# A Winograd-tiled pooling mixer: the first two products read inputs that are not yet normalized, and the second phase's weight operands are formed where they are needed

## The chip, the cores and the metric

The kernel runs on one core of a Trainium2 chip. A core has a matrix engine (TensorE, PE in the profile; PEld is its weight load), a vector engine (VectorE, DVE), a scalar engine (ScalarE, ACT), a general engine (GpSimd, POOL) that only issues transfers here, and a sync engine (SyncE, SP) that issues most of them. The engines run side by side and wait for one another through semaphores; each takes its own instructions in the order in which they were written for it. Matmul results land in eight PSUM banks of 128 x 512 floats, everything else lies in SBUF. The metric is the time of one execution in microseconds (us), as the median of several runs.

## The reference

One layer is computed (`DEPTH = 1`), the pooling mixer, on 4096 tokens of 1024 channels in float32:

```python
def pool_mixer(h, in_w, group_w, group_b, scale, out_w):
    u, gate = jnp.split(h @ in_w, 2, axis=-1)
    ug = u.reshape(b, s, POOL_GROUPS, POOL_GROUP_DIM)
    pooled = jnp.stack([trailing_mean(ug[:, :, g], w) for g, w in enumerate(POOL_WINDOWS)],
                       axis=2) - ug
    mixed = jnp.einsum('bsgc,gcd->bsgd', pooled, group_w) + group_b
    y = mixed.reshape(b, s, POOL_WIDTH) * scale * jax.nn.silu(gate)
    return y @ out_w

out = rms_norm(x + pool_mixer(rms_norm(x, norm_w), ...), final_norm_w)
```

`rms_norm` divides each token by the root of its mean square and multiplies by a weight per channel. `in_w` is 1024 x 2048 (a half for `u`, a half for the gate), `out_w` 1024 x 1024; there are four groups of 256 channels, with trailing windows of 2, 4, 8 and 16 tokens.

## The kernel before

**The arithmetic.** The factor per token of the first norm (here: the scale) is kept apart from the weight per channel, which is multiplied into the rows of `in_w`. The map of each group commutes with the mean over tokens, so it is folded into the `u` half of `in_w` once, at the start (`fold`, L284: `in_w` transposed times `group_w`, eight calls of 16 matmuls). Then the kernel has three phases, all made of blocked products in Winograd's form, seven products where plain blocking has eight:

- Phase a: 4 blocks of 1024 tokens, columns of groups 0 and 1. The input block is 2 x 2 (two halves of 512 tokens, two halves of the channels, called 11, 12, 21, 22), the weight is 2 x 2 (two halves of the channels; gate columns and folded columns).
- Phase b: the same blocks, columns of groups 2 and 3.
- Phase o: 8 blocks of 512 tokens times `out_w`, then the final norm.

A step is one product P1 to P7 of one block: 56 steps of 48 matmuls in phases a and b (order P1 P2 P6 P7 P5 P4 P3), 56 of 24 in phase o. Each float32 operand is split into a rounded high part (copied by ACT, L151) and a low part (subtracted by DVE, L145), and each product of two 128 x 128 by 128 x 512 blocks takes three matmuls (`mm3`, L457). The split input of a step lies in two of four `op` tiles, so a split can be made once the step before the last has been read out. P1 and P2 sum in the banks 0 to 3; P1 alone is also needed, so its four banks are copied to the banks 4 to 7 in between (`evict_in`, L564, ACT).

**The start.** SP loads the sources of the fold, then rows of `x` for the scales, then the transposed blocks. `square_row` (L316, ACT) gives the mean squares and `stats` (L325) four scales per partition for 512 tokens. `spread_rs` (L338) brings them to every partition: DVE forms a diagonal matrix in a weight tile not yet in use, two matmuls with ones (L351) write the bank 7, ACT copies it out. `normalize` (L365, DVE) multiplies an input half by it; then it is split, and GpSimd stores it, since phase b reads it again (`sd`).

**Later blocks.** For block b+1 the rows are loaded and squared during block b; the scales go to DRAM (`rd`) and come back broadcast to all partitions (`store_rs`, `load_rstd`), on the queue of SP. Pooling (`pool`, L503) is DVE work of one to four adds per group.

**Weights of phase b.** During blocks 1 and 2 of phase a, after P5, `make_wb` (L239) loads the gate rows of `in_w` and the folded weights `wvd`, forms all seven operands of one channel quarter pair (ACT scales, five DVE operations) and stores them in DRAM (`wbd`, 7 stores of 512 KB per call). After each product of the last block, `load_w` (L257) loads that product's operand for phase b from `wbd` and splits it into the weight tiles just set free.

**What sets the order.** The Python text gives the work in order of steps; a framework then places the instructions of all engines by its own estimates of time, keeping each engine's queue in the resulting order. `tc.high_priority()` moves a part ahead, `tc.issue_after(i)` holds one behind an instruction. Tiles for loads and temporaries come from two pools with the oldest free tile taken first (`Slots`), so a transfer waits for whoever read its tile last.

Of the kernel before, what the change touches and what calls it, by code (L numbers as in the profile page):

```python
# [60 lines left out]
def kernel(  # L61
# [91 lines left out]
    def split(dst, src):  # L153
# [3 lines left out]

    colt = const.tile([P, 24], F32, name="colt")
# [7 lines left out]
    wbd = {  # L166
        i: [dram.tile([P, 2, H], F32, name=f"wbd{i}_{h}") for h in range(2)]
        for i in range(P1, P7 + 1)
    }
# [270 lines left out]
    def split_in(q, b, i):  # L440
        s = xs[b]
        key = {P1: "11", P2: "12", P6: "2", P7: "21", P5: "11", P4: "22", P3: "12"}[i]
        t = split_halves(s[key], None if q else sd[b].get(i), b == 0)
# [5 lines left out]
        return t  # L449

# [15 lines left out]
    def product_in(i, t, sets, by_bank, between=None):  # L466
# [4 lines left out]
        for n, (h, ct) in enumerate(halves):  # L471
            if n == 5 and between:
                between()
# [90 lines left out]
    def evict_in(b, q, i, sets):  # L564
        ps = sets[bank_of[i]]
        last = None
        if i == P1:
# [282 lines left out]
    ru[0, 4] = load_wut(0, 4)  # L850
    g0.append(load_rows(in_w, 0, D))
    ru[0, 2] = load_wut(0, 2)
    g0.append(load_rows(in_w, 2, D))
    load_row(0, 0, 0)
    load_row(0, 0, 1)
    ru[0, 6] = load_wut(0, 6)
    load_row(0, 0, 2)
    load_row(0, 0, 3)
    ident = take(pool=early)
    nc.sync.dma_start(out=ident.rearrange("p a b -> p (a b)")[:, 0:P], in_=eye)  # L860
    gw[1] = load_group_w(1)
    v0, v1 = [None] * 2, [None] * 2
    for n, (h, k) in enumerate(chunks):
# [16 lines left out]
    give(gw[0])  # L880
    for h, k in chunks[1:]:
        ru[1, k] = load_wut(1, k)
# [14 lines left out]

    for n, (h, k) in enumerate(chunks):
        o = take(pool=early if n < 2 else early5)
        last = fold(1, k, gw[1], ru[1, k], banks[2 * (n % 2) : 2 * (n % 2) + 2], o)  # L900
# [193 lines left out]
```

## Time and profile before

| what | value |
|---|---|
| median of 3 runs (range) | 971.4 us (971.11 to 971.44) |
| the profiled execution: its time, its span | 973.14 us, 971.0 us |
| PE / PEld busy | 951.5 / 786.4 us |
| DVE / ACT / POOL busy | 745.6 / 452.2 / 6.7 us |
| granted TensorE clock, mean | 0.997 |
| read, written in DRAM | 116.50 MB, 67.12 MB |
| SP's queue, ACT's queue, GpSimd's queue (moved) | 163.71, 13.65, 6.29 MB |

The span is the time between the first and the last instruction; some 2 us of an execution lie around it. "Busy" counts overlapping instructions once, and matmuls are pipelined (one lasts 389 ns, but one ends every 227 ns in the even stretches), so a short wait of PE shows less idle time than it costs; the count of matmuls in a stretch tells more. A row of the timeline is: start, duration, engine, line, operation, output<-inputs, shape, count, and in brackets the idle time of the engine before it and what ended it.

### The profile page before, as it was taken

The numbers are of one execution on the slowest core, as the hardware profiler recorded it, in microseconds if no ns is written. First come the engines' busy times: TensorE is split into PE (matmuls) and PEld (weight loads), VectorE is DVE, ScalarE is ACT, GpSimd is POOL, SyncE is SP. The second block draws the span as 40 slices with busy tenths as digits, with TensorE's granted clock in tenths as the row PEclk, the third lists the DMA queues.
The fourth block names the chain that finished last, engine by engine and source line by source line (L and its number), as shares of the span: only waits on it lengthen the run. The fifth ranks groups of instructions, "written<-read, shape, count | busy, mean of one in ns | idle before, by whom it ended". The sixth has DMA issues, their size and how long they took to land.

```text
span 971.0 us, 11079 instructions
## 1 busy us (share of the span) xinstructions
PE 951.5 (98%) x4190; PEld 786.4 (81%) x4190; DVE 745.6 (77%) x907; ACT 452.2 (47%) x679; POOL 6.7 (1%) x16
## 2 busy tenths in 40 slices
PE   8899999989999999999999999999999999999996
PEld 7778888878877888888888888888888888888885
DVE  5696993886899794497598499599978677677675
ACT  4759438337545554345444435553424324324233
POOL 0100000000000000000000000000000000000000
PEclk9999999999999999999999999999999999999998
DMA  9964865977977624115714714646646446356022
GB/s 340 411 271 141 265 246 186 339 274 220 333 251 245 210 93 146 44 44 182 273 44 158 267 75 147 222 151 195 225 155 227 131 151 217 111 194 216 22 87 87
DMA packets 68933, 184.35 MB, mean 190 GB/s; under 512 B 6928, under 2 KB 24464, under 8 KB 68880
## 3 DMA queue, kind: packets, MB, share of 16 engines
q1 hardware_dynamic: 62976, 163.71, 49.1%
q10 hardware_dynamic: 4176, 13.65, 3.5%
q0 software_dynamic: 1728, 6.29, 1.6%
q8 instruction: 33, 0.54, 0.2%
q14 instruction: 20, 0.16, 0.1%
HBM read 116.50 MB, written 67.12 MB: 189 GB/s over the span
## 4 chain that ended last, share of the span: by engine, by line
PE 75%; DMA 10%; DVE 8%; ACT 4%; issue 1%; SPq 0%; ACTq 0%; DVEq 0%
PE bank L460 73%; DMA st<-in_in_w 3%; DMA rd<-rs 2%; DMA st<-rd 2%; DVE op L145 2%; PE bank L289 1%; DMA wbd<-vt 1%; DVE vt L142 1%; ACT vt L320 1%; DVE st L145 1%; DVE st L148 1%; DMA wbd<-st 1%; DMA early<-in_wut 1%; DVE st L546 1%; DVE vt L148 1%
## 5 line engine op out<-in xcount | busy, mean ns | idle before, releaser
L460 PE MATMUL bank<-op,w 128*128 128x512 f32 x2688 | 612.0, 389 | 5.6 <-DVE op L145 4.7
L460 PEld LDWEIGHTS bank<-op,w 128*128 128x128 f32 x2688 | 504.1, 188 | 112.7 <-DVE op L145 7.0
L460 PE MATMUL bank<-w,op 128*128 128x512 f32 (+1 forms) x1356 | 305.0, 387 | 0.0
L460 PEld LDWEIGHTS bank<-w,op 128*128 128x128 f32 x1356 | 253.1, 188 | 51.9
L151 ACT ACTIVATE op<-st 128x1024 fp32r<-128x1024 f32 x121 | 127.7, 1057 | 148.6 <-PE bank L460 108.2
L145 DVE TENSOR_TENSOR op<-st,op 128x1024 fp32r<-128x1024 f32 x121 | 147.3, 1223 | 58.9 <-ACT op L151 58.7
L142 DVE TENSOR_TENSOR vt<-vt 128x1028 f32<-128x1028 f32 (+6 forms) x72 | 88.0, 1235 | 1.7 <-DMA wbd<-vt 1.6
L151 ACT ACTIVATE op<-vt 128x1024 fp32r<-128x1024 f32 x45 | 47.4, 1059 | 81.1 <-PE bank L460 68.6
L142 DVE TENSOR_TENSOR st<-bank,st 128x512 f32<-128x512 f32 x76 | 52.0, 689 | 36.4 <-PE bank L460 34.3
L151 ACT ACTIVATE vt<-bank 128x512 f32<-128x512 f32 x94 | 54.8, 594 | 35.8 <-PE bank L460 34.2
L142 DVE TENSOR_TENSOR vt<-bank,vt 128x512 f32<-128x512 f32 (+1 forms) x85 | 56.7, 679 | 15.1 <-PE bank L460 8.7
L145 DVE TENSOR_TENSOR op<-vt,op 128x1024 fp32r<-128x1024 f32 x45 | 54.9, 1223 | 14.7 <-ACT op L151 14.6
L145 DVE TENSOR_TENSOR w<-st,w 128x1024 fp32r<-128x1024 f32 x32 | 39.1, 1224 | 21.4 <-ACT w L151 21.2
L151 ACT ACTIVATE w<-st 128x1024 fp32r<-128x1024 f32 x32 | 33.7, 1060 | 38.0 <-PE bank L460 28.7
L151 ACT ACTIVATE bank<-bank 128x512 f32<-128x512 f32 x48 | 27.9, 582 | 46.3 <-PE bank L460 29.9
L145 DVE TENSOR_TENSOR st<-st,st 128x1024 f32<-128x1024 f32 x38 | 46.2, 1224 | 2.4 <-DMA st<-wvd 1.9
L148 DVE TENSOR_TENSOR st<-st,st 128x1024 f32<-128x1024 f32 (+1 forms) x22 | 25.4, 1175 | 26.5 <-DMA st<-rd 18.3
L151 ACT ACTIVATE st<-bank 128x512 f32<-128x512 f32 x36 | 20.5, 594 | 20.0 <-DMA yd<-st 10.8
L541 DVE SCALAR_TENSOR_TENSOR vt<-vt,vt 128x1024 f32<-128x1024 f32 x24 | 29.4, 1226 | 0.1
L289 PE MATMUL bank<-early,early 128*128 128x256 f32 x128 | 28.3, 380 | 1.1 <-DVE st L297 1.1
L289 PEld LDWEIGHTS bank<-early,early 128*128 128x128 f32 x128 | 24.2, 190 | 4.7 <-DVE st L297 1.5
L142 DVE TENSOR_TENSOR st<-st,st 128x1024 f32<-128x1024 f32 x21 | 25.4, 1226 | 0.1
(109 smaller groups left out, 415.8 us busy)
## 6 DMA issues: line engine op xcount, KB each, us to landing
st<-in_x SPq DMA_DIRECT2D x32, 512.0 KB, 4.5
st<-sd SPq DMA_DIRECT2D x29, 512.0 KB, 4.5
vt<-in_x SPq DMA_DIRECT2D x27, 512.0 KB, 4.9
st<-in_xt SPq DMA_DIRECT2D x20, 512.0 KB, 5.9
st<-yd SPq DMA_DIRECT2D x19, 512.0 KB, 4.1
yd<-st SPq DMA_DIRECT2D x17, 512.0 KB, 3.5
out<-st SPq DMA_DIRECT2D x17, 512.0 KB, 5.1
sd<-st ACTq DMA_DIRECT2D x16, 512.0 KB, 5.6
```

The lines of the kernel that those rows point to most:

```text
L142: nc.vector.tensor_tensor(out=dst, in0=a, in1=b, op=ALU.add)
L145: nc.vector.tensor_tensor(out=dst, in0=a, in1=b, op=ALU.subtract)
L148: nc.vector.tensor_tensor(out=dst, in0=a, in1=b, op=ALU.mult)
L151: return nc.scalar.activation(dst, src, func)
L289: nc.tensor.matmul(ps2[kk][:, j * 256 : (j + 1) * 256], r[:, kk, 2 * j + t, :], g[:, 2 * j + t, :], start=(t == 0), stop=(t == 1),)
L320: nc.scalar.activation(u[:, 0], u[:, 0], AF.Square, accum_out=sums[b, half][:, j : j + 1])
L460: nc.tensor.matmul(ps, a, b, start=start and n == 0, stop=stop and n == 2, skip_group_check=True)
L541: nc.vector.scalar_tensor_tensor(out=s[:, :, at : at + H], in0=s[:, :, at : at + H], scalar=1.0 / win, in1=v[:, :, HIST:], op0=ALU.mult, o ...
L546: nc.vector.scalar_tensor_tensor(out=sg[:, j], in0=s[:, j, at : at + H], scalar=bias_c[2 * grp + j], in1=sg[:, j], op0=ALU.add, op1=ALU.mult,)
```

## The change

It has two parts, and some loads and squares of the start are put in another order with them.

1. In block 0 the inputs of P1 and P2 (11 and 12) are split as they are loaded (`raw`). The products are multiplied by the scales of the tokens when the banks are read out (`evict_in`: DVE multiplications in place of ACT copies; P2's sum then goes through the SiLU on ACT in two more operations). The inputs are normalized and stored afterwards (`normalize_raw`), for the products that need sums of them. The scales are spread at two points within the first product's text. All fold results are read out by ACT, none by DVE, and the transposed inputs are loaded ahead of the rows of `x`.
2. `wbd` is gone. For each product of phase b, `load_wb` loads the sources (gate rows, folded weights) one step ahead and `make_wb` forms and splits the operand in the steps 23 to 29, that is from P6 of the last block of phase a to P2 of the first of phase b. Sums are formed again where two products need them.

```diff
+    def split_negative(dst, src):
+        nc.scalar.activation(dst[:, 0], src, AF.Copy, scale=-1.0)
+        nc.vector.scalar_tensor_tensor(
+            out=dst[:, 1], in0=src, scalar=-1.0, in1=dst[:, 0].bitcast(F32),
+            op0=ALU.mult, op1=ALU.subtract,
+        )
...
-    def make_wb(h):
-        g0 = load_rows(in_w, 2 * h, D + H)
-        g1 = load_rows(in_w, 4 + 2 * h, D + H)
-        v0, v1 = take(), take()
-        nc.sync.dma_start(out=v0, in_=wvd[h])
-        nc.sync.dma_start(out=v1, in_=wvd[2 + h])
-        scale_rows(g0, pair(norm_c, h, 0))
-        scale_rows(g1, pair(norm_c, h, 1))
-        store_weights(wbd, h, g0, g1, v0, v1)
+    parts, t2 = {}, {}
+
+    def load_wb(i):
+        for h in range(2):
+            p = parts[i, h] = {}
+            if i in (P1, P6, P5):
+                p["11"] = load_rows(in_w, 2 * h, D + H)
+            if i in (P2, P4):
+                p["21"] = load_rows(in_w, 4 + 2 * h, D + H)
+            for name, k, used in (("12", h, (P6, P7, P5)), ("22", 2 + h, (P6, P7, P3))):
+                if i in used:
+                    p[name] = take()
+                    nc.sync.dma_start(out=p[name], in_=wvd[k])
+
+    def scaled(u, cs, other, op):
+        for j in range(2):
+            nc.vector.scalar_tensor_tensor(
+                out=u[:, j], in0=u[:, j], scalar=cs[j], in1=other[:, j], op0=ALU.mult, op1=op
+            )
+
+    def make_wb(i):
+        for h in range(2):
+            p = parts.pop((i, h))
+            top, bottom = pair(norm_c, h, 0), pair(norm_c, h, 1)
+            if i == P1:
+                split_scaled(w[i][h], p["11"], top)
+            elif i == P2:
+                split_scaled(w[i][h], p["21"], bottom)
+            elif i == P6:
+                sub(p["12"], p["22"], p["12"])
+                scaled(p["11"], top, p["12"], ALU.add)
+                t2[h] = p.pop("11")
+                split(w[i][h], t2[h])
+            elif i == P7:
+                sub(p["22"], p["22"], p["12"])
+                split(w[i][h], p["22"])
+            elif i == P5:
+                scaled(p["11"], top, p["12"], ALU.subtract)
+                split_negative(w[i][h], p["11"])
+            elif i == P4:
+                scaled(p["21"], bottom, t2[h], ALU.subtract)
+                split(w[i][h], p["21"])
+                give(t2.pop(h))
+            else:
+                split(w[i][h], p["22"])
+            for u in p.values():
+                give(u)
...
-            if q == 0:
+            if q == 0 and b > 0:
                 for u in s["11" if i == P1 else "12"]:
                     normalize(b, 0, u)
...
-        t = split_halves(s[key], None if q else sd[b].get(i), b == 0)
+        raw = b == 0 and i in (P1, P2)
+        t = split_halves(s[key], None if q or raw else sd[b].get(i), b == 0)
...
+    def normalize_raw(i):
+        for h, u in enumerate(xs[0]["11" if i == P1 else "12"]):
+            normalize(0, 0, u)
+            nc.gpsimd.dma_start(out=sd[0][i][h], in_=u)
...
-            if n == 5 and between:
-                between()
+            if between and n in between:
+                between[n]()
...
+        if i in (P1, P2) and b == 0 and q == 0:
+            if i == P2:
+                ev["11"] = [take() for _ in range(2)]
+            for c, u in enumerate(sets["y"] if i == P1 else cells(ev["11"])):
+                mul(u, ps[c], rstd[0][:, 0])
+            if i == P2:
+                for u in ev["11"]:
+                    last = copy(u, u, AF.Silu)
+        elif i == P1:
...
-        fold(0, k, gw[0], ru[0, k], banks[2 * (n % 2) : 2 * (n % 2) + 2], o, True)
+        fold(0, k, gw[0], ru[0, k], banks[2 * (n % 2) : 2 * (n % 2) + 2], o)
+        ru[1, k] = load_wut(1, k)
         if n == 0:
-            ru[1, 0] = load_wut(1, 0)
             load(0)
+            g0.append(load_rows(in_w, 2, D))
+            split_scaled(w[P1][0], g0[0], pair(norm_c, 0, 0))
         elif n == 1:
-            for hh in range(2):
-                split_scaled(w[P1][hh], g0[hh], pair(norm_c, hh, 0))
+            split_step(0)
         elif n == 2:
-            for j in range(4):
-                square_row(0, 0, j)
-            with tc.high_priority():
-                rs = stats(0, 0)
+            split_scaled(w[P1][1], g0[1], pair(norm_c, 1, 0))
+        if n > 1:
+            for j in range(2 * n - 4, 2 * n - 2):
+                load_row(0, 0, j)
...
-        if n == 1:
-            with tc.high_priority():
-                spread_rs(0, rs)
-            form(0)
-            split_step(0)
-            second_side(0)
-        elif n == 2:
-            behind = last.ins
+        if n < 2:
+            second_side(n)
+            for j in range(2 * n, 2 * n + 2):
+                square_row(0, 0, j)
+            if n == 1:
+                with tc.high_priority():
+                    rs[0] = stats(0, 0)
+        else:
+            for j in range(2 * n - 4, 2 * n - 2):
+                square_row(0, 1, j)
...
-    run(0, spread_second)
+    run(0, {1: lambda: spread(0), 5: lambda: spread(1)})
...
+    normalize_raw(P1)
+    for h in range(2):
+        for key in ("21", "22"):
+            normalize(0, 1, xs[0][key][h])
     form(2)
+    split_step(2)
     run(1)
-    split_step(2)
+    normalize_raw(P2)
...
+        since = n - (NB - 1) * len(ORDER_IN) - 2
+        if 0 <= since < len(ORDER_IN):
+            with tc.issue_after(evicted[0]):
+                make_wb(ORDER_IN[since])
+        if 0 <= since + 1 < len(ORDER_IN):
+            load_wb(ORDER_IN[since + 1])
...
-            if b == NB - 1:
-                load_w(wbd if kind == "a" else wod, i)
-            if i == P5:
-                if kind == "a" and b in (1, 2):
-                    make_wb(b - 1)
-                elif kind == "b" and b in (1, 2):
-                    make_wo(b - 1)
+            if kind == "b" and b == NB - 1:
+                load_w(wod, i)
+            if kind == "b" and b in (1, 2) and i == P5:
+                make_wo(b - 1)
```

More of the change, by code (lines that the diff above doesn't have):

```diff
@@ L165 @@
     wvd = [dram.tile([P, 2, H], F32, name=f"wvd{k}") for k in range(4)]
[L166 to L169, printed above, removed]
     wod = {
@@ L849 @@
     ru[0, 0] = load_wut(0, 0, by=1)
-    ru[0, 4] = load_wut(0, 4)
+    for h, k in chunks[1:]:
+        ru[0, k] = load_wut(0, k)
     g0.append(load_rows(in_w, 0, D))
[L852 to L858, printed above, removed]
+    gw[1] = load_group_w(1)
     ident = take(pool=early)
     nc.sync.dma_start(out=ident.rearrange("p a b -> p (a b)")[:, 0:P], in_=eye)
-    gw[1] = load_group_w(1)
     v0, v1 = [None] * 2, [None] * 2
@@ L896, in second_side, with spread @@
         split(w[P6][h], g0[h])
+    rs = [None] * 2
     for n, (h, k) in enumerate(chunks):
         o = take(pool=early if n < 2 else early5)
-        last = fold(1, k, gw[1], ru[1, k], banks[2 * (n % 2) : 2 * (n % 2) + 2], o)
+        fold(1, k, gw[1], ru[1, k], banks[2 * (n % 2) : 2 * (n % 2) + 2], o)
         nc.gpsimd.dma_start(out=wvd[k // 2], in_=o)
         give(o)
-        if n == 1:
-            with tc.high_priority():
-                spread_rs(0, rs)
-            form(0)
-            split_step(0)
-            second_side(0)
-        elif n == 2:
-            behind = last.ins
+        if n < 2:
[8 more added lines that the diff above has]
+                square_row(0, 1, j)
     give(gw[1])
     load(2)
-    with tc.issue_after(behind):
-        for j in range(4):
-            square_row(0, 1, j)
     with tc.high_priority():
-        rs = stats(0, 1)
-    def spread_second():
+        rs[1] = stats(0, 1)
+    def spread(half):
         with tc.high_priority():
-            spread_rs(1, rs)
-    run(0, spread_second)
+            spread_rs(half, rs[half])
+    run(0, {1: lambda: spread(0), 5: lambda: spread(1)})
     give(ident)
-    form(1)
     split_step(1)
```

6 lines of the change are left out of this document (1 added, 5 removed).

## The prediction

> **What bounds the kernel now.** I read the page first, then busy time by stretches, then PE's timeline of the stretches where it falls behind, then the queues that it waited for there. The page's first rows:
>
> ```profile
> span 971.0 us, 11079 instructions
> PE 951.5 (98%) x4190; PEld 786.4 (81%) x4190; DVE 745.6 (77%) x907; ACT 452.2 (47%) x679; POOL 6.7 (1%) x16
> ```
>
> PE is the bound, and the question is how often it falls behind. Busy time by stretches (PE's count in the first bracket):
>
> ```profile
> 39.70:60.00 20.30, 19.74 (x87) 15.81 (x85) 17.02 (x25) 13.89 (x23) 3.23 (x7) 1.00 1.03 416
> 60.00:140.00 80.00, 79.82 (x351) 65.30 (x350) 71.94 (x85) 48.40 (x74) 0.26 (x1) 1.00 0.62 207
> 39.70:320.00 280.30, 274.10 (x1200) 224.33 (x1199) 227.13 (x264) 161.77 (x254) 3.50 (x7) 1.00 0.75 259
> 320.00:960.00 640.00, 640.00 (x2826) 530.10 (x2825) 488.48 (x585) 264.24 (x381) 0.00 (x0) 1.00 0.43 149
> ```
>
> From 320 us on PE is never idle: 640/2826 = 0.2265 us per matmul, 10.87 us per step of 48. At that pace the 1200 matmuls of 39.7 to 320 need 271.8 us and took 280.3: 8.5 us lost, of which 0.6 before 60 us (87 need 19.7), 0.5 in 60 to 140 (351 need 79.5), so some 7.4 in 140 to 320. Nothing after 320 can get faster by this change. What it can reach is the time to the first product, these 8.5 us, and what it puts in anew. PE's timeline of the start:
>
> ```profile
> 7.30 13.97 PE L289 MATMUL bank<-early,early 128*128 128x256 f32 x64
> ...
> 22.38 3.69 PE L289 MATMUL bank<-early,early 128*128 128x256 f32 x16 [1.10 <-DVE st L297]
> 29.00 0.50 PE L351 MATMUL bank<-w,w 128*128 128x512 f32 x1 [2.94 <-DVE w L344]
> ...
> 30.00 10.09 PE L289 MATMUL bank<-early,early 128*128 128x256 f32 x46
> 39.74 9.00 PE L460 MATMUL bank<-op,w 128*128 128x512 f32 x38
> 49.29 0.50 PE L351 MATMUL bank<-w,w 128*128 128x512 f32 x1 [0.56 <-DVE w L344]
> ```
>
> The second half of the fold waits 1.1 us for an eviction by DVE, then 2.9 us at the spread of the scales. The later waits:
>
> ```profile
> 129.40 12.78 PE L460 MATMUL bank<-op,w 128*128 128x512 f32 x55 [0.18 <-DVE op L145]
> ...
> 198.24 12.30 PE L460 MATMUL bank<-op,w 128*128 128x512 f32 x53 [1.89 <-DVE op L145]
> 211.50 3.74 PE L460 MATMUL bank<-op,w 128*128 128x512 f32 x15 [0.96 <-ACT bank L151]
> ...
> 287.56 11.18 PE L460 MATMUL bank<-op,w 128*128 128x512 f32 x48 [2.06 <-DVE op L145]
> 299.30 3.94 PE L460 MATMUL bank<-op,w 128*128 128x512 f32 x16 [0.56 <-DVE op L145]
> ```
>
> They stand where blocks 2 and 3 begin. The recorded idle of the last four is 5.5 us. What DVE, ACT and SP did ahead of the first two (third column: engine; in brackets the idle time):
>
> ```profile
> 165.85 2.36 DVE L148 TENSOR_TENSOR st<-st,st 128x1024 f32<-128x1024 f32 x2 [6.82 <-DMA wbd<-st]
> 184.48 0.15 DVE L148 TENSOR_TENSOR rs<-rs,tmp 128x4 f32<-128x4 f32 x1
> 205.83 1.23 DVE L148 TENSOR_TENSOR st<-st,st 128x1024 f32<-128x1024 f32 x1 [3.10 <-DMA st<-rd]
> 210.86 0.58 ACT L151 ACTIVATE bank<-bank 128x512 f32<-128x512 f32 x1 [7.86 <-DMA sd<-vt]
> ```
>
> and, from the chain of waits, the two transfers that bring scales back:
>
> ```profile
> 192.11 6.54 DMA rd<-rs
> 198.71 7.09 DMA st<-rd
> ```
>
> DVE stands 6.8 us before a normalization because the scales come back through SP's queue in between `make_wb`'s loads and stores; its own operations then pile up; the next scales are ready at 184.6, leave at 192.1 and are back at 205.8; DVE waits for them again, ACT's stores of the results block ACT's copies of the banks, and PE waits for those.
>
> **The change part by part. Start.** Durations that I use:
>
> ```profile
> 22.08 1.28 ACT L186 ACT_TABLE_LOAD   x1
> 34.25 1.38 ACT L301 ACTIVATE early<-bank,colt 128x512 f32<-128x512 f32 x2
> 44.12 1.04 ACT L151 ACTIVATE op<-vt 128x1024 fp32r<-128x1024 f32 x1
> 48.25 0.19 ACT L151 ACTIVATE hl<-rs 128x4 fp32r<-128x4 f32 x1
> 49.76 1.41 DVE L206 SCALAR_TENSOR_TENSOR w<-st,colt,w 128x512 fp32r<-128x512 f32 x2
> 59.24 2.35 DVE L145 TENSOR_TENSOR early<-vt,st 128x1024 f32<-128x1024 f32 x2
> 77.95 3.12 ACT early L320 x6
> L142 DVE TENSOR_TENSOR st<-bank,st 128x512 f32<-128x512 f32 x76 | 52.0, 689 | 36.4 <-PE bank L460 34.3
> ```
>
> (A square with its sum: 3.12/3 = 1.04; a DVE operation of 1024 columns every 1.14 to 1.18, one of 512 with a scalar 0.7; a bank read by DVE 0.69, or 0.62 in a row, by ACT 0.6 to 0.7.)
>
> Removed from the path: nothing but evictions stands between the halves of the fold, and ACT makes these in time (two banks are always free). The first 64 fold matmuls end at 7.30 + 13.97 = 21.3, 0.218 each, 3.5 a fold; 64 more end at 35.2, so the first product starts at about 35.0 instead of 39.74: 4.7 us won. Its operands: the raw halves and the weights are loaded ahead of `x`, and their splits stand on ACT and DVE inside the first fold half, where DVE has lost its eight evictions.
>
> Put in its place: in the changed order of instructions the first spread stands on PE behind only 6 product matmuls, at 36.4 us. Its scales: the squares of the four rows stand on ACT between the fold's evictions, the last behind the second bank of the third fold of the second half (21.3 + 3 x 3.5 = 31.8; eviction to 32.4; square to 33.45); one more eviction to 34.2, a table load to 35.5, root and five small DVE operations at 0.2 to 36.8, the copy `hl` behind one more square at 36.95; from that copy to the spread matmul it was 49.29 - 48.25 = 1.04. So 38.0: PE waits 1.6, and 0.35 for the second spread matmul. From there DVE is one chain without a pause: the second spread matmul (0.5) ends at 39.2, ACT's copy of the bank (0.6) at 39.9, and until the sums for P6 stand two normalizations, four banks, two splits, the second spread, four half weight splits and small ones (12.8 us, to 52.7), then four normalizations and three sums (8.0, to 60.7); ACT's copy makes the operand of P6 ready at 61.9. PE has ended P2 at 38.9 + 89 x 0.2265 + 0.2 = 59.3, so it waits some 2.5 us, and 0.7 for the low part. P7 and P5 are met (0.1). Waits in all: 1.6 + 0.35 + 0.2 + 2.5 + 0.7 + 0.1 = 5.45. End of P5 after: 35.0 + 242 x 0.2265 + 5.45 = 95.3; before: 87 matmuls at 60.0 and 155 more, 95.1. The start gains 4.7 and gives it back: I take +0.4. Bounds: -3 if P6 does not wait; +3 if the scales take from the last square to the spread what they take now (the table load behind the last square began at 22.08, the spread at 29.0: 6.9 instead of my 4.55). The stores of the normalized halves move behind the fold's on GpSimd's queue; they are first read in phase b, and only DVE's later sums overwrite their tiles.
>
> **Blocks 2 and 3.** `make_wb` takes from them twice: ten DVE operations (11.8 us), eight ACT scalings, 8 loads and 14 stores. In the new order the store of the scales on SP is no longer behind stores that wait for DVE, and the splits of P1 stand ahead of the pooling work. Counting DVE's work from P4's last bank: one bank, five half-width operations of pooling, two splits, three normalizations and four sums (13.5 us, and some 2 of waiting for the scales) until the operand of P2 stands, and two steps are 21.7. So the waits of 198 to 299 go. The gain lies between 1.9 (only the wait of 198.24 goes) and 7.4 (all); I take 6.4, since 1 us may come back at P2 of block 1, where 129.40 waits without `make_wb`.
>
> **Phase change.** The 14 operands come from 22 loads of 512 KB, as many as now (8 sources, 14 `wbd`); only the 14 stores are gone. Added on DVE: four subtractions (4.7 us), twelve half-width scaled sums (8.4 at 0.7), some 0.7 for the eight half splits: 13.8 us in 290 to 375. The cover:
>
> ```profile
> 310.00:321.00 11.00, 11.00 (x51) 9.09 (x50) 6.37 (x6) 6.22 (x9) 0.00 (x0) 1.00 0.91 335
> 321.00:332.00 11.00, 11.00 (x50) 9.13 (x49) 6.96 (x8) 4.85 (x7) 0.00 (x0) 1.00 0.46 151
> 332.00:342.50 10.50, 10.50 (x48) 8.69 (x47) 10.43 (x12) 5.06 (x8) 0.00 (x0) 1.00 0.47 148
> 342.50:353.00 10.50, 10.50 (x48) 8.69 (x47) 10.18 (x12) 6.80 (x9) 0.00 (x0) 1.00 0.39 143
> 353.00:364.00 11.00, 11.00 (x50) 9.13 (x49) 11.00 (x11) 4.96 (x8) 0.00 (x0) 1.00 0.20 66
> 364.00:375.00 11.00, 11.00 (x50) 9.09 (x50) 7.47 (x10) 4.81 (x7) 0.00 (x0) 1.00 0.68 229
> ```
>
> DVE (third pair) is idle 12.6 us in these 65. It fits, barely: the tightest operand (P6 of phase b) stands behind about 25 full-width operations' worth that start at P4's end, 29 us, and three steps are 32.6. Loads wait on SP for tiles that DVE frees and DVE for the loads, with a step's slack. I take 0.1 lost; bounds 0 and 13.8.
>
> Sum: +0.4 - 6.4 + 0.1 = -5.9. The profiled execution took 973.14 (span 971.0 and 2.1 around it), so 967.2 for such a one; the median shown, 971.4, is 1.7 below it, and against that it is 965.5 us.
>
> **The rivals.** (1) The start costs 3 to 4 us: x rows late, small DVE operations late, and P6, P5 behind DVE. For it: the two rows of 22.38 and 29.00 show both waits now. Sum +3.5 - 6.4 + 0.1: 968.6. (2) Blocks 2 and 3 keep half their waits, because the scales still travel through DRAM (6.5 and 7.1 us above) and 129.40 shows a wait without `make_wb`: 968.7. (3) Slower: DVE's added work at the phase change comes ahead of splits that PE needs, in an order fixed beforehand, so that the idle 12.6 us are not where it stands. It decides from 5.9 us on; if two thirds of the 13.8 land on the path (9.1), 971.4 - 6.0 + 9.1 = 974.5. Against it: the splits stand a step ahead. (4) The change doesn't do what it says: the first product starts early and waits as long as before. For the start that is nearly my forecast; if the later waits stay too, 971.4 + 0.4 = 971.8. (5) PE's waits lower its clock. The rows:
>
> ```profile
> 20.00:30.00 10.00, 5.96 (x27) 4.57 (x27) 8.11 (x16) 5.85 (x9) 0.67 (x1) 1.00 1.04 397
> 960.00:971.00 11.00, 3.22 (x26) 2.97 (x24) 5.79 (x22) 4.99 (x13) 0.00 (x0) 0.78 0.45 167
> ```
>
> With idle times of 1.1 and 2.94 us the clock stayed at 1.00; at the end, with PE mostly idle, it fell to 0.78: 0.22 x 11 = 2.4 us of full clock. If a wait at P1 or P6 grows beyond 2.94 and costs that, 965.5 + 1 + 2.4 = 968.9. [...]
>
> **How the numbers follow.** Forecast 0.50, (1) 0.15, (2) 0.12, (3) 0.14, (4) 0.04, (5) 0.05. What a measurement can tell from no change is about 0.2%, 1.9 us, so faster means below 969.5. The forecast's own spread (its start between -3 and +3) keeps nearly all of it there: 0.48; (1), (2) and (5) two thirds, 0.21: faster 0.69. The rest of these, (4) and a little of the forecast make 0.15 within; (3) and the last of the others 0.16 slower. The range goes from 962.0 (start at its low bound) to 974.0: less than one in ten below, and most of (3)'s upper half above.
>
> **What would show it.** First product at 35 us; a wait of 1 to 2 us at the first spread (named DVE w) and of 2 to 3 at P6 (named ACT op or DVE op); some 242 matmuls done by 95 us; no idle PE at the starts of blocks 2 and 3; the scales' return on SP within 10 us of their making; 290 to 375 with DVE nearly full and PE at 50 matmuls per 11 us. I am wrong if PE loses more than 2 us in 290 to 390, if it waits over 3 us at P6, or if waits named DVE op remain at 180 to 300.

## The result, and the profile after

The changed kernel takes 965.9 us (median of 4, 964.4 to 966.9), the kernel before on the same chip 971.4 (971.1 to 971.6): ratio 0.9946, 95% interval 0.9931 to 0.9961, so 5.2 us faster (3.8 to 6.7 by the interval). More executions on another chip gave the same (0.9948, below). The profiled execution of the changed kernel took 964.39 us, 1.5 below its median, and that of the kernel before was 1.7 above its own; so the two traces differ by 8.4 us of span, and the medians by less. One execution of a kernel further down (two normalizations on GpSimd) took 2499 us, far from its other ten, and is left out of its ratio.

From the page of the changed kernel (span; busy time, share and count of each engine):

```profile
span 962.6 us, 11058 instructions
PE 949.7 (99%) x4190; PEld 785.5 (82%) x4190; DVE 748.4 (78%) x919; ACT 453.0 (47%) x677; POOL 6.7 (1%) x16
```

PE is idle 12.9 us of the span instead of 19.5. Where that went shows in busy time by stretches that all begin at 0; in the first bracket stands how many matmuls PE has done by then. First the kernel before, then the changed one; both have 4190 in all.

```profile
0.00:140.00 140.00, 133.77 (x578) 110.07 (x579) 113.18 (x146) 83.49 (x129) 6.72 (x16) 1.00 0.78 282
...
0.00:320.00 320.00, 308.31 (x1342) 253.30 (x1343) 251.34 (x301) 182.97 (x287) 6.72 (x16) 1.00 0.78 272
0.00:400.00 400.00, 388.31 (x1695) 319.56 (x1696) 303.36 (x355) 220.27 (x336) 6.72 (x16) 1.00 0.70 244
```

```profile
0.00:140.00 140.00, 134.97 (x587) 110.89 (x588) 113.95 (x147) 88.86 (x136) 6.72 (x16) 1.00 0.78 286
...
0.00:320.00 320.00, 314.97 (x1381) 259.94 (x1382) 244.69 (x302) 186.95 (x288) 6.72 (x16) 1.00 0.67 239
0.00:400.00 400.00, 394.78 (x1732) 325.68 (x1733) 310.25 (x373) 222.85 (x338) 6.72 (x16) 1.00 0.63 225
```

At 0.2265 us each: 9 matmuls ahead at 140 us (2.0 us), 39 at 320 (8.8, so 6.8 won between), 37 at 400 (8.4, so 0.5 given back at the phase change), and nothing after that. PE's timeline of the changed kernel (start, duration, line, operation, in brackets the idle time and what ended it) shows the start and the one wait of the phase change:

```profile
6.41 27.79 PE L334 MATMUL bank<-early,early 128*128 128x256 f32 x128
33.84 1.72 PE L512 MATMUL bank<-op,w 128*128 128x512 f32 x6
36.80 0.50 PE L396 MATMUL bank<-w,w 128*128 128x512 f32 x1 [1.24 <-DVE w L389]
...
60.88 39.41 PE L512 MATMUL bank<-op,w 128*128 128x512 f32 x171 [2.14 <-ACT op L151]
...
367.17 33.18 PE L512 MATMUL bank<-op,w 128*128 128x512 f32 x145 [0.19 <-DVE op L145]
```

The fold runs unbroken, the first product starts at 33.84 instead of 39.74, and two waits stand in its place, 1.24 at the first spread and 2.14 at P6. Between 140 and 320 us PE does not wait at all. The scales' trip of block 2 (SP's store and load, and DVE when they are back) is early:

```profile
176.87 0.42 SPq L381 DMA_DIRECT2D rd<-rs  x1
182.96 0.33 SPq L408 DMA_DIRECT2D st<-rd  x1
186.04 1.23 DVE L148 TENSOR_TENSOR st<-st,st 128x1024 f32<-128x1024 f32 x1 [4.22 <-DMA st<-rd]
```

It leaves 15 us sooner than the 192.11 of the kernel before and is back at 186.0 instead of 205.8.

### The profile page after: what moved, and what is told of

It is laid out like the page before. It is cut to its first block, busy times and chain, and to the rows that moved or that the text cites. A ratio compares the mean times of both kernels' runs of the same rounds, so it can differ in the third digit from the quotient of the medians.

```text
span 962.6 us, 11058 instructions
## 1 busy us (share of the span) xinstructions
PE 949.7 (99%) x4190; PEld 785.5 (82%) x4190; DVE 748.4 (78%) x919; ACT 453.0 (47%) x677; POOL 6.7 (1%) x16
## 4 chain that ended last, share of the span: by engine, by line
PE 78%; DVE 13%; DMA 5%; ACT 3%; issue 1%; DVEq 0%; SPq 0%; ACTq 0%
PE bank L512 75%; PE bank L334 2%; DVE op L145 2%; DVE vt L142 2%; DMA st<-wvd 2%; DVE st L148 1%; DVE st L145 1%; DMA rd<-rs 1%; DVE st L598 1%; DVE w L145 1%; DMA st<-rd 1%; DVE st L261 1%; DVE vt L145 1%; DVE w L209 1%; DVE st L142 1%
## 5 line engine op out<-in xcount | busy, mean ns | idle before, releaser
L151 ACT ACTIVATE op<-st 128x1024 fp32r<-128x1024 f32 x117 | 123.2, 1056 | 142.0 <-PE bank L512 112.2
L145 DVE TENSOR_TENSOR op<-st,op 128x1024 fp32r<-128x1024 f32 x117 | 141.5, 1217 | 38.7 <-ACT op L151 38.3
L151 ACT ACTIVATE op<-vt 128x1024 fp32r<-128x1024 f32 x49 | 51.8, 1059 | 92.2 <-PE bank L512 72.9
L142 DVE TENSOR_TENSOR vt<-vt 128x1024 f32<-128x1024 f32 (+6 forms) x72 | 87.7, 1227 | 0.1
L145 DVE TENSOR_TENSOR op<-vt,op 128x1024 fp32r<-128x1024 f32 x49 | 59.8, 1220 | 21.7 <-ACT op L151 21.7
L145 DVE TENSOR_TENSOR st<-st,st 128x1024 f32<-128x1024 f32 x35 | 42.3, 1217 | 13.0 <-DMA st<-wvd 11.2
L145 DVE TENSOR_TENSOR w<-st,w 128x1024 fp32r<-128x1024 f32 x22 | 26.5, 1220 | 16.4 <-ACT w L151 16.2
L148 DVE TENSOR_TENSOR st<-st,st 128x1024 f32<-128x1024 f32 (+1 forms) x18 | 20.4, 1160 | 19.6 <-DMA st<-rd 18.3
L151 ACT ACTIVATE w<-st 128x1024 fp32r<-128x1024 f32 x22 | 23.1, 1059 | 22.9 <-PE bank L512 15.4
L598 DVE SCALAR_TENSOR_TENSOR st<-vt,colt,st 128x512 f32<-128x512 f32 x36 | 25.6, 742 | 0.0
```

What stands on the lines that cost most here:

```text
L142: nc.vector.tensor_tensor(out=dst, in0=a, in1=b, op=ALU.add)
L145: nc.vector.tensor_tensor(out=dst, in0=a, in1=b, op=ALU.subtract)
L148: nc.vector.tensor_tensor(out=dst, in0=a, in1=b, op=ALU.mult)
L151: return nc.scalar.activation(dst, src, func)
L598: nc.vector.scalar_tensor_tensor(out=sg[:, j], in0=s[:, j, at : at + H], scalar=bias_c[2 * grp + j], in1=sg[:, j], op0=ALU.add, op1=ALU.mult,)
```

## The experiments

The twelve kernels ran on three chips, four together on each. The kernel before had medians of 972.5, 970.7 and 969.9 us there, so ratios are against it on the same chip, and times in us are compared within four.

### Which part brings the gain

**The new start alone**: the changed kernel with the old `make_wb`, its stores and `wbd` put back.

```
-                make_wb(ORDER_IN[since])
...
-            load_wb(ORDER_IN[since + 1])
...
+            if b == NB - 1:
+                load_w(wbd if kind == "a" else wod, i)
+            if i == P5 and kind == "a" and b in (1, 2):
+                make_wb(b - 1)
```

> The changed start with the old weight path (make_wb and its stores as before). My theory: the start as a whole is worth nothing: by the traces of before and after, 436 and 440 product matmuls are done at 140 us, 0.9 us apart, and the fold began 0.9 us earlier in the trace of after (6.41 against 7.30). So 971.4 within 1 us, and idle PE named DVE op or ACT bank still stands between 190 and 300 us, 4 to 6 us in all. Rival 1 (the start itself brings the gain and the rest follows from being early): 966 to 967, with those waits gone. Rival 2 (the start costs and the weights pay for it): 973 or more.

Measured: 972.0 against 972.5, ratio 0.9996 (0.9984 to 1.0007). The start by itself brings nothing that can be told, and its trace keeps 4.0 us of waits named DVE op in 190 to 302. (The counts that I gave ahead of this run were misread: at 140 us the traces of before and after have 432 and 441 product matmuls, nine apart and not four.) The trace, of the slowest of its twelve executions (969.9 to 974.7), also shows something new. The trace of this kernel has the same wait of 2.14 us at P6; here are its timeline at the two longest waits and 2 us stretches around the first (the third number from the end is the granted clock):

```profile
62.66 47.70 PE L469 MATMUL bank<-op,w 128*128 128x512 f32 x202 [2.14 <-ACT op L151]
...
199.83 89.06 PE L469 MATMUL bank<-op,w 128*128 128x512 f32 x378 [2.76 <-DVE op L145]
```

```profile
60.00:62.00 2.00, 0.52 (x3) 0.10 (x1) 2.00 (x3) 1.48 (x3) 0.53 (x1) 1.00 0.97 389
62.00:64.00 2.00, 1.34 (x3) 1.15 (x4) 2.00 (x4) 1.98 (x3) 0.00 (x0) 0.67 0.74 299
64.00:66.00 2.00, 2.00 (x6) 1.51 (x6) 2.00 (x4) 1.04 (x2) 0.00 (x0) 0.50 0.02 6
66.00:68.00 2.00, 2.00 (x10) 1.64 (x9) 2.00 (x3) 1.86 (x2) 0.00 (x0) 0.97 0.00 0
```

After a wait that cost the changed kernel 2.14 us and no more, the clock here is at half for some 3 us. More on that in the last section.

**The new weight path alone**: the kernel before with `load_wb` and the new `make_wb`, the reverse of the edit above on the old start.

> The old start with the new weight path (sources loaded and combined at the phase change). My theory: all of the gain, 965 to 966.5; no idle PE between 190 and 300 us; the two waits of the old start (1.1 and 2.9 us before 30 us) as before. Rival 1 (the start brings it): 970 to 971.5. Rival 2 (part of it hangs on the start): 967 to 969.

Measured: 970.3, ratio 0.9977 (0.9964 to 0.9990): 2.2 us, less than half of the gain. No wait is left between 140 and 320 us, as expected. But PE's timeline at the phase change, which has one wait of 0.19 in the changed kernel, has three here, and the stretch behind the last runs at a lower clock:

```profile
348.63 15.03 PE L503 MATMUL bank<-op,w 128*128 128x512 f32 x65 [0.75 <-DVE op L145]
363.89 7.34 PE L503 MATMUL bank<-op,w 128*128 128x512 f32 x31 [0.24 <-ACT bank L151]
373.51 26.87 PE L503 MATMUL bank<-op,w 128*128 128x512 f32 x110 [2.29 <-DVE op L145]
```

```profile
370.00:380.00 10.00, 7.71 (x27) 5.88 (x26) 10.00 (x10) 5.67 (x8) 0.00 (x0) 0.83 0.51 179
```

From 320 to 400 us it does 330 matmuls where the kernel before does 355: 5.7 us, given back out of what blocks 2 and 3 won. Some 1.7 us of it is the halved clock (0.83 over these 10 us); this execution too was the slowest of its twelve (966.6 to 972.4).

**The changed kernel again**, unedited, with more executions.

> The changed kernel itself, unedited, against the kernel before on one chip with more executions of both. Old start with new weights gave 970.3 and new start with old weights 972.0 against 972.5, so apart the parts bring 2.2 and 0.5 us, together 2.7. My theory: they do not add up, since the new start also takes away waits at the phase change that the old start has with the new weights (3.2 us of idle PE and a halved clock after it): 965.5 to 967.5 here, 5 to 7 us below the kernel before, and at most 0.5 us of idle PE in 320 to 400. Rival: they add up and the earlier comparison was a lucky one: 969.5 to 970.5.

Measured: 965.65 against 970.65, ratio 0.9948 (0.9930 to 0.9966), with 0.47 us of idle PE in 320 to 400. So the parts do not add up: 0.5 and 2.2 us apart, 5.0 together. The 2.3 us between are hardly more than the three intervals together leave open; it is the stretch from 320 to 400, with 351 matmuls here and 330 with the weight path alone, that carries the claim. The new start is worth little where it stands, and more 300 us later.

**The sums left out**: the old start with the new weight path, as in the second experiment, but with the four subtractions and twelve scaled sums of `make_wb` deleted, loads and splits kept.

```
-                sub(p["12"], p["22"], p["12"])
-                scaled(p["11"], top, p["12"], ALU.add)
...
-                scaled(p["21"], bottom, t2[h], ALU.subtract)
```

> The old start with the new weight path, its four subtractions and twelve scaled sums of the phase change left out (13.1 us of DVE; the second phase's weights are other numbers), with the same loads and splits. With them this kernel lost 3.3 us of idle PE in 340 to 375 and more to a halved clock. My theory (DVE's added work uses up the cover, and the loads that wait for tiles DVE has not freed do the rest): these waits go, 964.5 to 966.5. Rival (the loads of the sources are late by themselves, since they are issued only a step ahead): the waits stay, 969 to 971.

Measured: 966.0, ratio 0.9965 (0.9953 to 0.9977). There is no idle PE between 320 and 400, 354 matmuls against 330; PE runs through from 50.91 to past 420 us:

```profile
50.91 374.47 PE L498 MATMUL bank<-op,w 128*128 128x512 f32 x1649
```

The interval overlaps with that of the kernel with the sums (a different chip, whose kernel before was 2.6 us lower), so it is the trace that decides: the added work on DVE causes the waits of the phase change. Why the new start avoids them is seen only in part. DVE's waits in 300 to 375 us (total, times, longest), old start first, changed kernel second:

```profile
DVE st L145 <- DMA st<-wvd: 14.5, 3, 5.8
```

```profile
DVE st L145 <- DMA st<-wvd: 7.7, 2, 4.6
```

With the old start DVE stands 6.8 us longer for loads of the sources, which SP issues when a tile comes free. Which tiles these are follows from a rotation that the start sets; that this is what differs was not tried on its own and stays open.

### What the waits of blocks 2 and 3 were

**No stores**: the kernel before; `make_wb` loads, scales and combines, and stores nothing. The phase change loads as much as before, but halves of `wvd` in place of `wbd`.

```
-        store_weights(wbd, h, g0, g1, v0, v1)
+        us = combine(g0, g1, v0, v1)
+        for u in us.values():
+            give(u)
...
-                load_w(wbd if kind == "a" else wod, i)
+                load_w(wvp if kind == "a" else wod, i)
```

> The kernel before; make_wb still loads, scales and combines in blocks 1 and 2, but stores nothing (14 stores of 512 KB gone), and the phase change loads halves of wvd in place of wbd, so its weights are other numbers. It separates DVE's and ACT's added work from the queue. My theory (the scales' store and return stand on SP's queue behind stores that wait for DVE): the waits of 190 to 300 go almost wholly, 966 to 967.5. Rival (DVE's ten operations are too much for the two steps, whatever the queue does): the waits stay, 970 to 971.5.

Measured: 966.25, ratio 0.9944 (0.9928 to 0.9960), no wait of PE between 140 and 400; from 160 to 310 us it is one piece:

```profile
159.73 150.44 PE L459 MATMUL bank<-op,w 128*128 128x512 f32 x663
```

With all of its arithmetic on DVE and ACT, the kernel before without these 14 stores is as fast as the changed kernel.

**The stores on GpSimd's queue**:

```
-            nc.sync.dma_start(out=dst[i][h], in_=u)
+            q.dma_start(out=dst[i][h], in_=u)
...
-        store_weights(wbd, h, g0, g1, v0, v1)
+        store_weights(wbd, h, g0, g1, v0, v1, nc.gpsimd)
```

> The kernel before; make_wb as before, but its 14 stores are issued by GpSimd instead of SP, so that no wait for DVE stands on SP's queue ahead of the scales, while the bytes and DVE's work stay. My theory: like the run without stores within 1 us, 966 to 968, waits of 190 to 300 nearly gone. Rival (the bytes themselves, 7.3 MB, slow the scales' trip): 969 to 971.5 where the run without stores is fast. Rival (DVE's work): both stay at 970 to 971.5.

Measured: 977.1, ratio 1.0054 (1.0035 to 1.0073), slower than before, with 7.7 us of waits in 140 to 320. SP's queue is free of the stores, and yet this is what SP and DVE show:

```profile
187.08 0.63 SPq L337 DMA_DIRECT2D rd<-rs  x1
193.82 0.33 SPq L364 DMA_DIRECT2D st<-rd  x1
```

```profile
189.57 1.23 DVE L148 TENSOR_TENSOR st<-st,st 128x1024 f32<-128x1024 f32 x1 [4.60 <-DMA st<-in_xt]
```

```profile
SPq L394 <- DMA wbd<-st: 7.1, 2, 6.4
```

SP now stands 6.4 us before a load of `x^T`, because its tile is still being stored; the scales leave behind that load, and DVE waits for the load itself. The scales still leave 5 us sooner than in the kernel before (187.08 for 192.11), so the stores on SP's queue did hold them; it did not help, as the load of `x^T` is now what DVE waits for.

**No arithmetic**: the kernel before; `make_wb` issues its 8 loads and 14 stores, but writes the loaded halves out as they are.

```
-        scale_rows(g0, pair(norm_c, h, 0))
-        scale_rows(g1, pair(norm_c, h, 1))
-        store_weights(wbd, h, g0, g1, v0, v1)
+        for i, u in zip((P1, P2, P6, P7, P5, P4, P3), (g0, g1, g0, v0, g1, v1, v0)):
+            nc.sync.dma_start(out=wbd[i][h], in_=u)
...
```

> The kernel before; make_wb issues all of its loads and 14 stores but neither scales nor combines (the stores write the loaded halves, so the second phase's weights are other numbers). Without the stores but with the arithmetic, the waits of 190 to 300 us were gone; with the stores on GpSimd's queue they stayed, at 7.7 us. My theory as it now stands (tiles stay taken until their stores have left, loads queued on SP wait for those tiles, and the scales' trip stands behind these loads): stores that need not wait for DVE leave at once, so the waits fall to 2 us or less, 966 to 968. Rival (14 stores of 512 KB on top of the other transfers are the cause, whatever they wait for): the waits stay at 4 to 8 us, 970 or more.

Measured: 973.5, ratio 1.0045 (1.0028 to 1.0062): my theory falls, the rival holds. DVE is busy 9.7 us less in 140 to 320 (128.5 for 138.2, with 148 operations for 156; `combine` in `make_wb` has four DVE operations, not five as I wrote of the kernel before, so eight in all and not ten), the stores wait for DVE no longer, only for their own loads (6.8 us of SP's waits in 150 to 230), and the waits are there, 4.0 us of idle in 208 to 292:

```profile
208.14 80.55 PE L461 MATMUL bank<-op,w 128*128 128x512 f32 x347 [2.62 <-DVE op L145]
```

```profile
183.28 0.55 SPq L337 DMA_DIRECT2D rd<-rs  x1
194.31 0.33 SPq L364 DMA_DIRECT2D st<-rd  x1
```

```profile
197.78 1.23 DVE L148 TENSOR_TENSOR st<-st,st 128x1024 f32<-128x1024 f32 x1 [4.93 <-DMA st<-rd]
```

```profile
160.00:180.00 20.00, 20.00 (x90) 16.58 (x89) 13.40 (x19) 10.28 (x19) 0.00 (x0) 1.00 0.99 340
180.00:200.00 20.00, 20.00 (x90) 16.56 (x89) 11.99 (x14) 6.28 (x7) 0.00 (x0) 1.00 0.86 293
```

The scales leave early enough, but 11 us pass until their load is issued; SP waits 8.1 us of these for 2 KB to land. The last number but one may say why: the DMA engines are 0.99 and 0.86 busy in these 40 us, where the changed kernel has 0.73 and 0.50; but the run without stores has 0.68 and 0.83, so this is argued. What the three runs settle: the 14 stores make the waits; DVE's arithmetic does not. The way is not the same in all of them. From the scales' store to the issue of their load it takes 6.6 us in the kernel before, 6.7 with the stores on GpSimd's queue, 6.2 without stores and 6.1 in the changed kernel; the first two send them late (at 192.1 and 187.1, for 183.0 and 176.9). Only here they leave in time (183.3) and the trip itself is long (11.0). Whether it is the busy DMA engines or the tiles that a store holds was not separated: the run without stores has neither these transfers nor tiles held by them.

### The waits of the start

**The first spread later**: behind 12 product matmuls instead of 6 (`newest` holds the last product matmul).

```
-    run(0, {1: lambda: spread(0), 5: lambda: spread(1)})
+    run(0, {2: lambda: spread(0), 5: lambda: spread(1)})
...
+            with tc.issue_after(newest[0].ins):
+                nc.tensor.matmul(
+                    banks[7], ones, r[:, s, 0], start=s == 0, stop=s == 1, skip_group_check=True
+                )
```

> The changed kernel with the two matmuls of the first spread put behind 12 product matmuls instead of 6 (the second spread's stay near where they were). PE then has work while the scales are made. My theory (DVE's chain from the scales on sets when P6 can start, PE's own wait does not): the wait at the first spread (1.2 us) goes to 0 to 0.3, the wait at P6 grows from 2.1 by as much, to 3.0 to 3.6, and the time stays within 0.5 us of the changed kernel, or is 1 us longer where the longer wait halves the clock. Rival (the two waits are independent): 1.2 us faster, P6's wait stays at 2.1.

Measured: 965.9 against 965.65 for the changed kernel on the same chip (ratio to before 0.9950, 0.9931 to 0.9968). The wait at the spread is gone, the one at P6 grew, though by less than I expected (to 2.65, not to 3.0 and more), and behind it the clock was at half (0.50 from 62.38 to 64.88, 10 matmuls fewer in 60 to 140 us):

```profile
61.88 48.35 PE L515 MATMUL bank<-op,w 128*128 128x512 f32 x205 [2.65 <-ACT op L151]
```

**Two normalizations on GpSimd**:

```
...
+                r = rstd[0][:, 0].unsqueeze(1).to_broadcast([P, 2, H])
+                engine.tensor_tensor(out=u, in0=u, in1=r, op=ALU.mult)
...
-    normalize_raw(P1)
+    normalize_raw(P1, nc.gpsimd)
```

> The changed kernel with the two normalizations of block 0's first halves (normalize_raw for P1, 2 x 1.2 us of DVE) on GpSimd, which is idle there. My theory (P6's operand stands behind DVE's chain): DVE reaches the sums 2.4 us sooner, the wait at P6 falls from 2.1 to under 0.5, first-spread wait unchanged: 2 us faster than the changed kernel, more if a wait of 2.1 us halves the clock in some executions. Rival 1 (GpSimd is so slow, or slows DVE so much, that the sums wait for it): the wait at P6 stays or grows, named POOL. Rival 2 (something else, such as loads, is late next): the wait stays at 1 to 2 us under another name.

Measured: 968.1, 2.5 us slower than the changed kernel, where I had expected 2 us faster. The wait at P6 is nearly gone (0.27 and 0.35), but one of 2.2 us stands at the second spread, and one of 0.84 at P5. While GpSimd multiplies, one of DVE's small operations on the scales takes 1.87 us where it takes 0.15 in the changed kernel:

```profile
39.88 4.76 POOL L504 TENSOR_TENSOR st<-st,st 128x1024 f32<-128x1024 f32 x2 [1.33 <-ACT st L151]
```

```profile
42.79 1.87 DVE L148 TENSOR_TENSOR tmp<-rs,ms 128x4 f32<-128x4 f32 x1
```

```profile
46.78 0.47 PE L396 MATMUL bank<-w,w 128*128 128x512 f32 x1 [2.21 <-DVE w L389]
```

**Both edits together**:

> Both edits: first spread behind 12 product matmuls, the two normalizations on GpSimd. My theory: the wait at the first spread goes (1.2 us), the wait at P6 stays at 1 us or less, 2.5 to 3.5 us faster than the changed kernel. Rivals as for the two parts.

Measured: 969.4, slower still, where I had expected the fastest of all. With PE further on when it meets it, the wait at the second spread is 4.1 us, and the clock behind it is at half (0.50 from 47.19 to 49.69).

**The first half of P6's operand first**: no work added or removed.

```
-    for h in range(2):
...
+    def operand(h):
+        for key in ("21", "22"):
+            normalize(0, 1, s0[key][h])
+        sub(s0["21"][h], s0["11"][h], s0["21"][h])
+        sub(s0["2"][h], s0["22"][h], s0["21"][h])
+        split_up.setdefault(2, []).extend(split_halves([s0["2"][h]]))
+    with tc.high_priority():
+        operand(0)
+    operand(1)
```

> The changed kernel with the first half of P6's operand made first: its two normalizations and two differences ahead of those of the second half on DVE, and its copy ahead of P7's on ACT. No work is added or taken away. My theory (P6 waits for the place of its operand in DVE's chain, which ran normalizations of both halves and four differences before the first copy): the wait of 2.1 us at P6 goes to 0.3 or less; 2 us faster than the changed kernel, 963.5 to 964.2, a little more where that wait halves the clock. Rival (the next thing is late by nearly as much: the low part, or the second half's operand): a wait of 1 to 2 us under the name DVE op, gain under 1 us.

Measured: 966.4, ratio 0.9961 (0.9949 to 0.9973), no better than the changed kernel's 0.9948, where I had expected 2 us. The wait at P6 is gone, and one of the same size stands two steps later, at P5:

```profile
85.49 14.79 PE L512 MATMUL bank<-op,w 128*128 128x512 f32 x57 [2.39 <-DVE op L145]
```

DVE is busy 37.4 of the 40 us from 60 to 100 in this trace and 37.1 in the changed kernel's. So the order at P6 seems only to choose the step at which PE meets the backlog.

**That, and the first spread later**:

> The same, and the first spread's matmuls behind 12 product matmuls. Alone, that took away the 1.2 us at the first spread and P6's wait grew instead (2.65, with the time unchanged). My theory: with slack at P6 the 1.2 us now stay won: 962.3 to 963.2. Rival (they come back at P6 or P7): no faster than the run with only the first half first.

Measured: 965.8, ratio 0.9962 (0.9949 to 0.9976); waits of 0.61 at 59.84 and 2.38 at 84.27. The rival holds, but for the place: they come back at P5, not at P6 or P7. None of these beats the changed kernel.

## Where the prediction was right, and where not

**The time.** Forecast 965.5 (962 to 974), measured 965.9. The change of -5.9 us stands against -5.2 by the ratio, but the terms hit less well than the sum. By the traces they are -2.0, -6.8 and +0.5, together -8.3; that the median still fell within 0.4 us of the forecast is in part luck, since both profiled executions stood off their medians (below).

**Start, +0.4 (bounds -3 to +3): mis-sized.** The trace has -2.0 at 140 us. Of it 0.9 is no work of the change: the fold began at 6.41 instead of 7.30, since the warm-up ended sooner (it took 5.11 us for 6.00, last section). The other 1.1 comes mostly from how I counted the kernel before, not from the waits. From the first product to the end of P5 I forecast 242 x 0.2265 + 5.45 = 60.3 us, and the changed kernel took 60.2 (33.84 to 94.0). The two recorded waits add up to less (1.24 + 2.14), but a wait shows less idle time than it costs (a matmul of 128x512 lasts 389 ns in the changed kernel too, and one ends every 227), and the spread's own matmuls take time (0.50 us each). For the kernel before I took its 87 matmuls at 60 us as products and had P5 end at 95.1; four of the 87 belong to the fold and the spread, 83 are products, and P5 ended at 96.0. Mechanism and places were right: DVE's chain from the scales on, first at the spread, then at P6. The experiment with the new start alone puts the part at nothing, -0.5 us with 1.1 either way; behind the wait at P6, which this part brings, the clock was at half in the trace of that experiment, for 1.7 us more, and at 1.00 in the two traces of the changed kernel (last section). What the part did not see is that DVE's backlog outlasts P6.

**Blocks 2 and 3, -6.4 (bounds -1.9 to -7.4): the size was right, the reason in part wrong.** 30 matmuls, 6.8 us. The prediction named three things: the scales between `make_wb`'s transfers, its stores on SP waiting for DVE, and DVE's operations that pile up (ten by my count, eight in the kernel). The run without arithmetic keeps the waits, the one without stores loses them, and stores on another queue than SP's make them longer. So the stores are the cause and DVE's work is not; their place on SP's queue delays the scales by 5 us, but taking it away did not take the waits away. The 1 us that I held back for P2 of block 1 was not needed: 0.18 us stands there, as before.

**Phase change, 0.1 (bounds 0 to 13.8): right for this kernel, with no margin.** 0.19 us in one trace, 0.47 in the other. "It fits, barely" rested on counting 13.8 us of work against 12.6 of idle time; DVE is busy 13.5 us more in 320 to 400 (65.6 for 52.0). The same work on the old start did not fit: 3.3 us of waits and a lowered clock behind them (0.76 over 7.1 us). That is the mechanism of rival (3), below the point from which it decides.

**Rival (5), the clock: the condition was wrong.** I let it begin beyond 2.94 us, since that wait had cost nothing. The clock fell behind a wait of 2.14 us (the new start alone) and stayed at 1.00 behind one of 3.20 (the stores on GpSimd's queue): the length alone does not decide, and what else does was not shown (last section).

**The median.** I carried over the 1.7 us between profiled execution and median of the kernel before. The changed kernel's profiled execution stood 1.5 on the other side, so that conversion was no better than its spread. Without it the forecast for a profiled execution was 967.2, and 964.4 was measured.

What would have shown it wrong did not occur: 0.2 us idle in 290 to 390, 2.1 at P6, no wait in 180 to 300. The 242 matmuls forecast for 95 us were done by then.

## What to carry to other kernels

When an engine has a backlog, moving one operand forward can move the wait to another operand, as it did here (2.14 us at P6, then 2.39 at P5); less work on that engine took a wait away (the sums left out). A round trip through DRAM cost more here than its arithmetic (966.25 us without the stores, 973.5 without the arithmetic): SP stood 6.4 us before a load whose tile was still being stored (the stores on GpSimd's queue), the DMA engines were 0.99 and 0.86 busy for 40 us (no arithmetic), and what suffered was another transfer that everything waits for, the scales or a load of `x^T`. And two parts of a change should be tried apart and together: here they made 0.5, 2.2 and 5.0 us.

## What the runs showed of the hardware

**Behind waits of the same length PE's clock was at half in some executions and not in others.** Over the fourteen traces PE waits 20 times for 2.06 to 4.12 us between the start of the fold and its last stretch; behind 11 of these the granted clock falls (to 0.50 to 0.65 as a mean of 2.5 us), behind 9 it stays at 1.00. Behind 12 waits of 1.1 to 1.9 us it never falls. The same wait of 2.14 us is in the traces of the changed kernel (1.00, twice) and of its start alone (0.50). Here are the 7.1 us behind it in the changed kernel:

```profile
60.78:67.88 7.10, 6.98 (x29) 5.48 (x30) 7.10 (x9) 4.41 (x5) 0.53 (x1) 1.00 0.22 91
```

and in the new start alone, with those behind its wait of 2.76 us:

```profile
62.56:69.66 7.10, 7.00 (x24) 5.65 (x25) 7.10 (x9) 4.40 (x5) 0.53 (x1) 0.76 0.15 62
199.73:206.83 7.10, 7.00 (x18) 5.52 (x19) 3.72 (x5) 0.84 (x4) 0.00 (x0) 0.55 1.00 369
```

The length alone does not decide: behind 2.94 us in the kernel before and 3.20 with the stores on GpSimd's queue the clock stayed at 1.00, behind 2.14 it fell. What else does was not shown. Ten of the 11 falls leave 0.76 over these 7.1 us, 0.24 x 7.1 = 1.7 us lost; one leaves 0.55, 3.2 us lost. So the price of such a wait was its length plus 0, 1.7 or, once, 3.2 us, and a kernel with several of them may vary by it: the kernel before ranged from 969.1 to 975.0 us in 23 executions beside 964.8 to 967.4 in 6 of the changed one. That the clock makes this spread is argued from the price, not shown execution by execution; it can't be all of it, since the profiled execution of the kernel before, 1.7 us above its median, has no such fall before PE's last stretch.

**The pace of the warm-up changed earlier in some executions than in others.** The 14 warm-up matmuls took 5.0 to 6.3 us over the fourteen traces, though all begin at 1.45 or 1.46, and the fold starts right behind them in all but one. From the second on they start 0.43 us apart up to 5.03 in the changed kernel and up to 6.74 in the kernel before, and 0.23 apart behind that (after one step of 0.32 in the kernel before; a row's 1.00 tells nothing there, as these two traces have no record of the clock before 5.01 and 6.92). Here the changed kernel and the run with two normalizations on GpSimd:

```profile
1.45 5.11 PE L900 MATMUL bank<-op 128*128 128x512 f32 x14 [1.45 <-DVE op L898]
```

```profile
1.46 6.30 PE L904 MATMUL bank<-op 128*128 128x512 f32 x14 [1.46 <-DVE op L902]
```

The 1.2 us between them shift all that follows (the fold starts at 6.41 and 7.59); comparing two traces, one takes that off first.

**Some of DVE's operations took longer while GpSimd multiplied.** While GpSimd's two multiplications ran (2.4 us each, where DVE takes 1.2), a DVE operation of 128x4 with two inputs in SBUF took 1.87 us instead of 0.15, and 1.82 in the other run with this edit. It ended at 44.66, GpSimd's second multiplication at 44.64. A scaling of 128x4 with one input took 0.40 and 1.40 us in these two runs instead of 0.16. The multiplication of a bank that ran in the same stretch, with one input in PSUM, took its usual 0.70, and a reciprocal of 128x4 0.18. What sets these operations apart was not shown.
